# First matrices of two small networks: plain float32 products in four column quarters instead of split fp32r products

## The chip, the core and the metric

The kernel runs on one core of a Trainium2 chip. The core's engines each take their instructions in order from a queue of their own: TensorE (PE) multiplies matrices and keeps its result in PSUM, VectorE (DVE) and ScalarE (ACT) do arithmetic, GpSimd (POOL) does small work beside them, and SyncE (SP) issues the DMA transfers. An engine waits for another by a semaphore. PE's weight loads are shown as an engine of their own, PEld. The metric is the device time of one execution in microseconds (us), as the median of several runs.

## The reference, cut to what matters

A model of two blocks runs over 256 positions of 1024 channels in float32. The first block does, for each of two layers, a gated feed-forward, a mixing stage with three kinds of attention, and a second feed-forward. The second block (gated linear attention, attention on a memory, a mixture of experts) is not touched by the change. In the mixing stage one kind of attention reads compressed keys and values:

```
blocks = t[:, cmp_idx] + cmp_pos[:, None, :]                     # 15 blocks of 32 positions
blocks = blocks.transpose(0, 3, 1, 2, 4).reshape(B, G, n_cmp, CMP_LEN * Dh)   # G=2 groups, 2048 long
return jax.nn.silu(blocks @ w1) @ w2                             # w1: 2048 x 256, w2: 256 x 64
kc = rms_norm(compress(k_cmp, cmp_k_w1, cmp_k_w2), k_norm)
vc = compress(v_cmp, cmp_v_w1, cmp_v_w2)
```

So there are two small networks per layer, one for keys and one for values. Each multiplies 30 rows (2 groups x 15 blocks) of length 2048 with a first matrix of 2048 x 256, which is 2 MB.

## The kernel before

**Weights.** All weights stream from memory in units of at most 128 x 1024 numbers (512 KB), in the order of a list of requests (`mixing_requests`, L726, for a mixing stage). A request names a matrix, its first column, its width and, optionally, more. `load_ahead` (L265) issues a unit's DMA as soon as a room is free. `pump` (L277) splits loaded units in order: ACT writes the high part `whi` in the format fp32r (L311), DVE the rest `wlo` = raw - `whi` (L285), and the raw room becomes free. There are 5 rooms for raw units and 14 for the halves of 7 split units (`ST`); rooms that no split unit wants are given to the raw units (`wanted_spare`, L253). A unit marked as whole is not split: it stays in its raw room, `Taken.whole` (L338) hands it out, and `close` (L344) frees the room after its last product. Before the change only the experts' weights are whole; `pump` does not split ahead over a whole unit that is still open.

**Products.** An ordinary product of an activation block with a weight block is three fp32r matmuls, high by high, high by low, low by high (`mm3`, L357 to L360). `linear` (L386) goes over a request's units and both halves of the positions, and calls `tick` after each. Whole units are multiplied in plain float32, and the experts (L1936, L1961) put two products into the two halves of PE's 128 columns. Compressed values (L957) use quarters of 32 columns.

**The order of the work.** Every engine's order is the order in which the Python program issues instructions. Side work is written as generators. `tick` (L95) moves each running generator on to its next `yield`, starts at most one queued generator whose predecessors have ended, and lets `pump` split one unit. So the side work of a tick stands on PE, DVE and ACT between two pieces of the main products.

**The mixing stage.** The main line multiplies w_in in the requests D, E, F, B, A, C (L1162 to L1171), whose generators `post_D` to `post_C` normalize and transpose. `blocks` (L858) builds for each network the matrix X of its 16 blocks of 128 rows and 30 columns, and splits X as well (L890 on ACT, L891 on DVE). Then come `hidden(Xk)` and `hidden(Xv)` (L895), the products with the first matrices, 4 units each:

```python
for k in W.ks(u):
    for i, w in enumerate(W(k)):        # whi, wlo
        nc.tensor.matmul(p, X[0][k // 8][:, k % 8 * 60:k % 8 * 60 + 60], w, ...)
```

The stationary operand has 60 columns: the 30 of X's high part and the 30 of its low part, interleaved. The 60 rows of the result are added in pairs by a product with the constant `sums` (L915, in `squashed`, L908), between ACT's copy L911 and the silu (L918, L921). `compressed_keys` (L923) goes on with L929, L933 to L946, `compressed_values` (L950) with L957 and DVE's L960. After `hidden` come the gate products (`gate`, L1183: 8 ticks each, four of them), and beside them, one started per tick, four `sliding` (L1069 first), two `compressed` (L1011 first) and sixteen `selected_window` generators. The PSUM banks of the tags `mm`, `tp` and `accB` are two each. `finish(*heads)` at L1222 waits in ticks until they have all ended; then the merge follows.

**Small things.** Ring tiles (`ring`, L739) are eight buffers of 128 x 512. `sums` is made on POOL in the first feed-forward (L683 to L687).

Of the kernel before, what the change touches and what calls it, by code (L numbers as in the profile page):

```python
# [10 lines left out]
FT = mybir.dt.float32  # L11
FR = mybir.dt.float32r
I32 = mybir.dt.int32
AF = mybir.ActivationFunctionType
OP = mybir.AluOpType
# [54 lines left out]
def the_kernel(  # L70
# [115 lines left out]
    @contextmanager  # L186
    def stream(raw_slots, unit_bufs, requests):

        with tc.tile_pool(name="w", bufs=1, reuse_waits="tile") as wp:
            units, asked = [], []
            for w, c0, n, *pool in requests:
                ws = w if isinstance(w, tuple) else (w,)
                kt = ws[0].shape[0] // P
                per = min(kt, UNIT // n)
                asked.append((len(units), -(-kt // per) * len(ws), per, kt, n, len(ws)))
                for i, k0 in enumerate(range(0, kt, per)):
                    for m in ws:  # L200
                        units.append((m, c0, n, k0, min(per, kt - k0), bool(pool) and i % 4 in pool[0],
                                      isinstance(w, tuple)))
            now.update(room=unit_bufs, units=units, asked=asked, loads=[], parts=[], half=[], closed=0, open=0, busy=[])
            x_rooms[:] = [(wp, f"x{h}", True) for h in range(NH)]
            place_x()
            now["spare"] = [(wp, f"w{i}", True) for i in range(2 * unit_bufs)]
            with rooms(wp, raw_slots):
                yield
            assert not asked and now["closed"] == len(units)
# [67 lines left out]
    def pump(most=1, hurry=False, upto=None):  # L277


        units, parts, half = now["units"], now["parts"], now["half"]  # L280

        def second():
            if half:
                _, r, hi, lo, eng, at = half.pop()
                eng.tensor_sub(lo, r, hi.bitcast(FT))  # L285
                now["busy"].remove(at)
                used(at)

        load_ahead()
        while len(parts) < len(units) and (most > 0 if upto is None else len(parts) <= upto):  # L290
            *_, on_pool, whole = units[len(parts)]
            if len(parts) == len(now["loads"]):
                assert upto is None, "no room"
                break
            if whole:
                parts.append(None)
                continue
            if upto is None and any(whole for *_, whole in units[now["closed"]:len(parts)]):
                break
            if len(now["spare"]) < 2 + 2 * (upto is None):  # L300
                assert upto is None, "no room"
                break
            if hurry and not on_pool:
                return
            second()
            r, at = now["loads"][len(parts)]
            m, n = r.shape[1:]
            mine = [now["spare"].pop(0) for _ in range(2)]
            hi, lo = (block(at2, [UNIT], FR, t)[:, :m * n].rearrange("p (k n) -> p k n", n=n)
                      for at2, t in zip(mine, ("whi", "wlo")))  # L310
            nc.scalar.activation(hi, r, AF.Copy)  # L311
            half.append((len(parts), r, hi, lo, nc.gpsimd if on_pool else nc.vector, at))
            parts.append((hi, lo, mine))
            now["open"] += 1
            most -= 1
            load_ahead()
        if upto is None and most > 0 and not hurry or upto is not None and half and half[0][0] == upto:
            second()
# [321 lines left out]
    def mixing_constants(fb, tmp):  # L640
# [6 lines left out]
        dmul = fb.tile([P, P], FT, name="dmul")  # L647
        dadd = fb.tile([P, P], FT, name="dadd")
        rowm = fb.tile([P, 1], FT, name="rowm")
        sums = fb.tile([60, 30], FT, name="sums")  # L650
        mine = fb.tile([P, 4], FT, name="mine")
        nsink = fb.tile([P, 8], FT, name="nsink")
        pcp = fb.tile([P, 2, 16], FT, name="pcp")
# [7 lines left out]
        def load():  # L661
# [18 lines left out]
            nc.gpsimd.affine_select(rowm, rowm, pattern=[[0, 1]], compare_op=OP.is_ge, fill=0.0, base=-(CMPL - 1),  # L680
                                    channel_multiplier=1)

            nc.gpsimd.memset(sums, 1.0)  # L683
            nc.gpsimd.affine_select(sums, sums, pattern=[[-2, 30]], compare_op=OP.is_ge, fill=0.0, base=0,
                                    channel_multiplier=1)
            nc.gpsimd.affine_select(sums, sums, pattern=[[2, 30]], compare_op=OP.is_ge, fill=0.0, base=1,
                                    channel_multiplier=-1)  # L687
            nc.gpsimd.memset(mine, 1.0)
            nc.gpsimd.affine_select(mine, mine, pattern=[[-32, 4]], compare_op=OP.is_ge, fill=0.0, base=0,
                                    channel_multiplier=1)  # L690
# [35 lines left out]
    def mixing_requests(l):  # L726
        W = w_in[l]
        gate = lambda b, j: (W, 2584 + b * D + j * 512, 512)
        up = lambda j: [(w[l], j * 512, 512) for w in (w_up_nsa, w_up_sb, w_up_swa)]
        return [(W, 1304, 512), (W, 1816, 512), (W, 2328, 256), (W, 512, 512), (W, 0, 512), (W, 1024, 280),  # L730
                (nsa_cmp_k_w1[l], 0, 256), (nsa_cmp_v_w1[l], 0, 256), *(gate(b, 0) for b in range(3)), gate(0, 1),
                *up(0), gate(1, 1), gate(2, 1), *up(1), *square(w_out[l])]

    def mixing(l, cs, xt, rs, ready, start):
        nbias, tri, nones, dmul, dadd, rowm, sums, mine, nsink, pcp = cs
        nxt = start()
        with tc.tile_pool(name=f"mix{l}", bufs=1, reuse_waits="tile") as mp:

            def ring():  # L739
                return mp.tile([P, 512], FT, name="gt", tag="gt", bufs=8)  # L740
# [117 lines left out]
            def blocks(c, into, *after):  # L858
                while any(g in active for g in after):
                    yield  # L860
                X = ring()[:, :480].rearrange("p (j n) -> p j n", n=30)
                T2 = ring()[:, :256].rearrange("p (g m) -> p g m", g=NG)
                kds = []
                for h in range(NH):
# [18 lines left out]
                        nc.vector.tensor_add(X[:, 8 * o:8 * o + 8, g * NCMP:(g + 1) * NCMP], v,  # L883
                                             pcp[:, 8 * o:8 * o + 8, None].to_broadcast([P, 8, NCMP]))
                yield
                both = [mp.tile([P, 512], FR, name="gt", tag="gt", bufs=8)[:, :480] for _ in range(2)]
                for i, t in enumerate(both):

                    xh, xl = (t.rearrange("p (j n a) -> p j n a", n=30, a=2)[:, :, :, a] for a in range(2))
                    nc.scalar.activation(xh, X[:, 8 * i:8 * i + 8], AF.Copy)  # L890
                    nc.vector.tensor_sub(xl, X[:, 8 * i:8 * i + 8], xh.bitcast(FT))  # L891
                into.append(both)
                yield

            def hidden(X):  # L895

                W = Taken()
                p = bank("accB")[:60, :256]
                for u in range(W.count):
                    for k in W.ks(u):  # L900
                        for i, w in enumerate(W(k)):
                            nc.tensor.matmul(p, X[0][k // 8][:, k % 8 * 60:k % 8 * 60 + 60], w, start=i == k == 0,
                                             stop=i == 1 and k == W.kt - 1)
                    W.close(1)
                    tick()
                return p

            def squashed(p, o):  # L908

                half = t2()[:60, :256]  # L910
                nc.scalar.activation(half, p, AF.Copy, scale=0.5)  # L911
                yield
                tp = tbank()[:, :2, :30]
                for i in range(2):
                    nc.tensor.matmul(tp[:, i], half[:, i * P:(i + 1) * P], sums, start=True, stop=True)  # L915
                yield
                th = t2()[:, :60].rearrange("p (c n) -> p c n", n=30)
                nc.scalar.activation(th, tp, AF.Tanh)  # L918
# [1203 lines left out]
```

## Time and profile before

| | us |
|---|---|
| median of 3 runs | 2220.94 |
| lowest and highest run | 2216.73, 2223.05 |
| the profiled execution | 2218.42 |
| its span, first to last instruction | 2216.7 |
| mean granted clock of TensorE | 0.993 of full |
| mixing stage of layer 0, the part from request C on | from 275 us |
| the same of layer 1 | from 900 us |

In a row of the timeline the columns are the start, the time taken (from the first start to the last end, where several are merged), the engine, the line, the operation, what it writes and reads, its shape, how many, and in brackets the engine's idle time before it with what ended it. A matmul's time goes on after the next one has started, so the rate is read from starts.

### The profile page before, as it was taken

Reading aid. Unit: us, or ns where it says so; the run is one execution under the profiler, and the core shown is the slowest. Engines: PE = TensorE matmul, PEld = TensorE weight load, DVE = VectorE, ACT = ScalarE, POOL = GpSimd, SP = SyncE. Lnnn points to the kernel's source line nnn. Section 1 sums busy time; section 2 is a strip of 40 time slices with the busy share of each in tenths; the row PEclk is TensorE's granted clock in tenths of the full one; section 3 lists DMA queues with packets and bytes.
Section 4 is the critical chain, followed back from the end, with each engine's and each line's share of the span. In section 5 each row is a group of like instructions: output and inputs, shape, how many; then the busy total and the mean of one; then the engine's idle time right before and its main releaser. Section 6 shows DMA issues by size and latency. Waiting matters only on the chain. (4 is left out here: it accounts for less than half of the span.)

```text
span 2216.7 us, 29473 instructions
## 1 busy us (share of the span) xinstructions
PE 2132.8 (96%) x11117; PEld 1569.8 (71%) x11117; DVE 1139.0 (51%) x2022; ACT 910.7 (41%) x1448; POOL 177.0 (8%) x230
## 2 busy tenths in 40 slices
PE   8999989999999999899999999998999999989997
PEld 7778878788888888788788887873333687953332
DVE  6545786654554547875554457651111558441112
ACT  5435655454454447564544454531111454421111
POOL 1000200200000002101100001101000102010000
PEclk9999999999999999999999999999999999999999
DMA  7655553555546555535666464778998946589996
GB/s 249 195 177 153 163 153 110 175 183 186 181 156 210 188 172 154 162 105 158 224 205 194 153 186 159 249 251 307 393 394 300 353 126 219 185 308 381 395 393 246
DMA packets 240076, 490.49 MB, mean 221 GB/s; under 512 B 17538, under 2 KB 44850, under 8 KB 239922
## 3 DMA queue, kind: packets, MB, share of 16 engines
q1 hardware_dynamic: 239634, 487.42, 65.1%
q8 instruction: 92, 1.51, 0.3%
q10 hardware_dynamic: 288, 1.05, 0.1%
q14 instruction: 62, 0.51, 0.1%
HBM read 487.34 MB, written 1.07 MB: 220 GB/s over the span
## 5 line engine op out<-in xcount | busy, mean ns | idle before, releaser
L285 DVE TENSOR_TENSOR wlo<-raw,whi 128x1024 fp32r<-128x1024 f32 x524 | 633.8, 1227 | 300.7 <-ACT whi L311 297.9
L311 ACT ACTIVATE whi<-raw 128x1024 fp32r<-128x1024 f32 x524 | 540.7, 1051 | 299.8 <-PE tp L360 117.5
L1936 PE MATMUL mm<-raw,xg 128*64 128x512 f32 x1024 | 242.7, 602 | 7.9 <-PEq L1992 7.2
L358 PE MATMUL accB<-whi,xt 128*128 128x512 f32 (+3 forms) x448 | 176.2, 393 | 0.0
L360 PE MATMUL accB<-whi,xt 128*128 128x512 f32 (+3 forms) x448 | 166.0, 370 | 0.0
L359 PE MATMUL accB<-wlo,xt 128*128 128x512 f32 (+3 forms) x448 | 165.8, 370 | 0.0
L1936 PEld LDWEIGHTS mm<-raw,xg 128*64 128x64 f32 x1024 | 69.6, 137 | 132.8 <-issue 121.5
L358 PE MATMUL tp<-whi,xt 128*128 128x512 f32 (+1 forms) x384 | 143.4, 373 | 0.0
L360 PE MATMUL tp<-whi,xt 128*128 128x512 f32 (+1 forms) x384 | 143.4, 373 | 0.0
L359 PE MATMUL tp<-wlo,xt 128*128 128x512 f32 (+1 forms) x384 | 142.7, 372 | 0.0
L358 PE MATMUL mm<-whi,xt 128*128 128x512 f32 (+1 forms) x320 | 121.0, 378 | 1.4 <-DVE nbias L720 0.7
L1961 PE MATMUL mm<-raw,t 128*64 128x512 f32 x512 | 119.3, 607 | 0.5 <-DMA raw<-in_w_down_dram 0.5
L360 PE MATMUL mm<-whi,xt 128*128 128x512 f32 (+1 forms) x320 | 118.3, 370 | 0.0
L359 PE MATMUL mm<-wlo,xt 128*128 128x512 f32 (+1 forms) x320 | 117.7, 368 | 0.0
L1941 ACT ACTIVATE t<-mm 128x512 f32<-128x512 f32 x32 | 19.1, 597 | 187.5 <-PE mm L1936 187.5
L360 PEld LDWEIGHTS accB<-whi,xt 128*128 128x128 f32 x448 | 84.5, 189 | 15.1
L358 PEld LDWEIGHTS accB<-whi,xt 128*128 128x128 f32 x448 | 84.6, 189 | 13.6 <-issue 1.0
L359 PEld LDWEIGHTS accB<-wlo,xt 128*128 128x128 f32 x448 | 84.8, 189 | 11.8
L1870 DVE TENSOR_SCALAR back<-tp 128x256 fp32r<-128x256 f32 x32 | 13.6, 424 | 149.2 <-PE tp L1867 149.2
L610 DVE SCALAR_TENSOR_TENSOR t<-tp,ss,t 128x512 f32<-128x512 f32 (+1 forms) x48 | 33.8, 704 | 104.2 <-PE tp L360 104.2
L359 PEld LDWEIGHTS tp<-wlo,xt 128*128 128x128 f32 x384 | 72.1, 188 | 13.5
L360 PEld LDWEIGHTS tp<-whi,xt 128*128 128x128 f32 x384 | 72.1, 188 | 13.2
(520 smaller groups left out, 4007.7 us busy)
## 6 DMA issues: line engine op xcount, KB each, us to landing
raw<-in_w_gate_dram SPq DMA_DIRECT2D x128, 512.0 KB
raw<-in_w_up_dram SPq DMA_DIRECT2D x128, 512.0 KB
raw<-in_w_down_dram SPq DMA_DIRECT2D x128, 512.0 KB
raw<-in_w_in_dram SPq DMA_DIRECT2D x120, 512.0 KB
raw<-in_ffn_w_gate_dram SPq DMA_DIRECT2D x88, 512.0 KB
raw<-in_ffn_w_up_dram SPq DMA_DIRECT2D x88, 512.0 KB
raw<-in_ffn_w_down_dram SPq DMA_DIRECT2D x88, 512.0 KB
raw<-in_w_out_dram SPq DMA_DIRECT2D x32, 512.0 KB
```

The costliest lines, as they stand in the source:

```text
L285: eng.tensor_sub(lo, r, hi.bitcast(FT))
L311: nc.scalar.activation(hi, r, AF.Copy)
L358: nc.tensor.matmul(o, xh, wh, start=first, stop=False)
L359: nc.tensor.matmul(o, xh, wl, start=False, stop=False)
L360: nc.tensor.matmul(o, xl, wh, start=False, stop=last)
L610: nc.vector.scalar_tensor_tensor(ss[h], o, factor(h), ss[h], op0=OP.mult, op1=OP.mult)
L1870: nc.vector.tensor_scalar(bk, tp, 0.0, None, op0=OP.is_gt)
L1936: nc.tensor.matmul(p[half(i)], xgs[e // 4][k // 4][:, k % 4, e % 4], W.whole(k, i), start=k == 0, stop=k == KD - 1)
L1941: nc.scalar.activation(c[e], p, AF.Copy)
L1961: nc.tensor.matmul(p[half(j)], uu[e][:, f], W.whole(f)[:, j * 512:(j + 1) * 512], start=f == 0, stop=f == 3)
```

## The change

The two first matrices are requested with the mark "alone": their units are not split, but `pump` goes on splitting units behind them. `hidden` multiplies the raw blocks in plain float32. The four blocks k of a unit go to four quarters of 32 columns, so that the result has 128 rows, four partial sums of 32 rows, and it ticks after every second unit. X is kept whole, 32 columns wide, with the last two set to zero by POOL; its split and the two ring tiles for it are gone, and with them the last `yield` of `blocks`. `squashed` works on 128 rows, and `sums` becomes a 128 x 32 matrix that adds the four quarters, made from the identity matrix by one DVE reduction.

```diff
@@ stream
-                        units.append((m, c0, n, k0, min(per, kt - k0), bool(pool) and i % 4 in pool[0],
-                                      isinstance(w, tuple)))
+                        units.append((m, c0, n, k0, min(per, kt - k0), False, "alone" if pool else isinstance(w, tuple)))
@@ pump
-            if upto is None and any(whole for *_, whole in units[now["closed"]:len(parts)]):
+            if upto is None and any(whole is True for *_, whole in units[now["closed"]:len(parts)]):
                 break
@@ mixing_constants
-        sums = fb.tile([60, 30], FT, name="sums")
+        sums = fb.tile([P, 32], FT, name="sums")
...
-            nc.gpsimd.memset(sums, 1.0)
-            nc.gpsimd.affine_select(sums, sums, pattern=[[-2, 30]], compare_op=OP.is_ge, fill=0.0, base=0,
-                                    channel_multiplier=1)
-            nc.gpsimd.affine_select(sums, sums, pattern=[[2, 30]], compare_op=OP.is_ge, fill=0.0, base=1,
-                                    channel_multiplier=-1)
+            nc.vector.tensor_reduce(sums, ident.rearrange("p (i n) -> p n i", n=32), axis=AX.X, op=OP.add)
@@ mixing_requests
-                (nsa_cmp_k_w1[l], 0, 256), (nsa_cmp_v_w1[l], 0, 256), *(gate(b, 0) for b in range(3)), gate(0, 1),
+                (nsa_cmp_k_w1[l], 0, 256, "alone"), (nsa_cmp_v_w1[l], 0, 256, "alone"), *(gate(b, 0) for b in range(3)), gate(0, 1),
@@ blocks
-                X = ring()[:, :480].rearrange("p (j n) -> p j n", n=30)
+                X = ring().rearrange("p (j n) -> p j n", n=32)
+                nc.gpsimd.memset(X[:, :, 30:], 0.0)
...
-                both = [mp.tile([P, 512], FR, name="gt", tag="gt", bufs=8)[:, :480] for _ in range(2)]
-                for i, t in enumerate(both):
-
-                    xh, xl = (t.rearrange("p (j n a) -> p j n a", n=30, a=2)[:, :, :, a] for a in range(2))
-                    nc.scalar.activation(xh, X[:, 8 * i:8 * i + 8], AF.Copy)
-                    nc.vector.tensor_sub(xl, X[:, 8 * i:8 * i + 8], xh.bitcast(FT))
-                into.append(both)
-                yield
+                into.append(X)
@@ hidden
-                p = bank("accB")[:60, :256]
+                p = bank("accB")[:, :256]
                 for u in range(W.count):
-                    for k in W.ks(u):
-                        for i, w in enumerate(W(k)):
-                            nc.tensor.matmul(p, X[0][k // 8][:, k % 8 * 60:k % 8 * 60 + 60], w, start=i == k == 0,
-                                             stop=i == 1 and k == W.kt - 1)
+                    for i, k in enumerate(W.ks(u)):
+                        nc.tensor.matmul(p[32 * i:32 * i + 32], X[0][:, k], W.whole(k), start=u == 0,
+                                         stop=u == W.count - 1)
                     W.close(1)
-                    tick()
+                    if u % 2:
+                        tick()
@@ squashed
-                half = t2()[:60, :256]
+                half = t2()[:, :256]
...
-                    nc.tensor.matmul(tp[:, i], half[:, i * P:(i + 1) * P], sums, start=True, stop=True)
+                    nc.tensor.matmul(tp[:, i], half[:, i * P:(i + 1) * P], sums[:, :30], start=True, stop=True)
```

## Rows read from the trace of the kernel before

**Rows 1.** The page, part 1: busy time, share of the span, instructions.
```profile
PE 2132.8 (96%) x11117; PEld 1569.8 (71%) x11117; DVE 1139.0 (51%) x2022; ACT 910.7 (41%) x1448; POOL 177.0 (8%) x230
```
**Rows 2.** Busy time by stretch of the span, with granted clock, DMA share and GB/s.
```profile
core 0: us, PE busy (x) PEld busy (x) DVE busy (x) ACT busy (x) POOL busy (x), PEclk, DMA share, GB/s
270.00:282.00 12.00, 10.31 (x80) 9.26 (x79) 11.03 (x23) 5.24 (x11) 4.12 (x2) 1.00 0.27 88
282.00:300.00 18.00, 14.16 (x111) 12.38 (x110) 17.07 (x43) 12.36 (x28) 3.42 (x3) 1.00 0.68 197
300.00:312.00 12.00, 10.18 (x77) 7.79 (x76) 10.02 (x42) 6.44 (x23) 0.63 (x2) 0.94 0.59 190
...
895.00:907.00 12.00, 10.32 (x81) 9.29 (x80) 11.06 (x22) 5.24 (x12) 4.11 (x2) 1.00 0.31 89
907.00:925.00 18.00, 15.23 (x109) 13.76 (x108) 16.86 (x45) 12.03 (x28) 2.42 (x3) 0.91 0.72 214
925.00:937.00 12.00, 10.18 (x80) 7.65 (x78) 10.05 (x42) 6.35 (x23) 0.61 (x2) 1.00 0.52 161
...
330.00:360.00 30.00, 30.00 (x190) 25.05 (x189) 24.49 (x99) 19.12 (x57) 0.00 (x0) 1.00 0.33 106
```
**Rows 3.** PE's waits from 270 to 312 us: total, times, longest.
```profile
PE tp L433 <- DVE t L757: 1.3, 1, 1.3
PE tp L915 <- ACT t L911: 1.2, 1, 1.2
PE mm L1011 <- DVE vc L960: 1.2, 1, 1.2
PE mm L929 <- DVE HT L921: 1.0, 1, 1.0
PE mm L1069 <- DVE kc L934: 0.9, 1, 0.9
PE tp L994 <- DVE kcT L946: 0.7, 1, 0.7
PE accA L1144 <- ACT gt L1133: 0.6, 1, 0.6
PE tp L873 <- DVE qT L818: 0.3, 1, 0.3
```
**Rows 4.** Timeline of PE: `hidden`'s records, first and 24th, and two of layer 1.
```profile
284.38 0.36 PE L902 MATMUL accB<-whi,gt 128*60 128x256 f32 x1
287.17 0.28 PE L902 MATMUL accB<-wlo,gt 128*60 128x256 f32 x1
...
919.00 0.42 PE L902 MATMUL accB<-whi,gt 128*60 128x256 f32 x1
919.21 0.42 PE L902 MATMUL accB<-wlo,gt 128*60 128x256 f32 x1
```
**Rows 5.** Plain float32: one line's records, its weight loads in time, L957's records by stretch.
```profile
L1936 PE MATMUL mm<-raw,xg x1024: 592/592/1116, 1502.3 to 2192.5; 128*64 128x512 f32 x171
...
1600.98 0.14 PEld L1936 LDWEIGHTS mm<-raw,xg 128*64 128x64 f32 x2 [0.28 <-issue]
1601.41 0.14 PEld L1936 LDWEIGHTS mm<-raw,xg 128*64 128x64 f32 x2 [0.29 <-issue]
...
307.79:308.02 0.23, 0.22 (x16) 0.22 (x16) 1.00 0.22 80
```
**Rows 6.** The page, part 5: the splits (count, busy, mean ns, idle before).
```profile
L285 DVE TENSOR_TENSOR wlo<-raw,whi 128x1024 fp32r<-128x1024 f32 x524 | 633.8, 1227 | 300.7 <-ACT whi L311 297.9
L311 ACT ACTIVATE whi<-raw 128x1024 fp32r<-128x1024 f32 x524 | 540.7, 1051 | 299.8 <-PE tp L360 117.5
```
**Rows 7.** Timelines of DVE (first two) and ACT.
```profile
276.06 0.73 DVE L891 TENSOR_TENSOR gt<-gt 128x240 fp32r<-128x240 f32 x2 [0.81 <-ACT gt L890]
276.70 0.69 DVE L757 TENSOR_TENSOR t<-t,hr 128x512 f32<-128x512 f32 x1
...
288.23 2.94 ACT L311 ACTIVATE whi<-raw 128x1024 fp32r<-128x1024 f32 x3
```
**Rows 8.** A memset on POOL (ns min/median/max).
```profile
L796 POOL MEMSET HV<- x2: 198/198/198, 214.8 to 839.6; 128x128 f32 x2
```
**Rows 9.** One more stretch, columns as in rows 2.
```profile
309.80:313.50 3.70, 3.70 (x14) 2.68 (x14) 2.77 (x10) 1.67 (x4) 0.00 (x0) 0.62 0.01 2
```

## The prediction

> **What bounds the kernel now.** I read the page first. TensorE (PE) is busy for 96% of the span [rows 1], so a change pays if it takes PE time away or fills an idle stretch of PE. Then I cut the two mixing stages, one per layer, into stretches [rows 2]. Between 330 and 360 us, where the gates are multiplied, PE has no idle time at all. Before that it has: PE is busy 10.31 of 12 us, 14.16 of 18 and 10.18 of 12 in layer 0, and 10.32 of 12, 15.23 of 18, 10.18 of 12 in layer 1. That is 7.3 and 6.3 us idle, and these are the stretches the change edits. In the middle one of layer 0 DVE is busy 17.07 of 18 us, so DVE queues there, and PE waits for what stands in that queue. The list of PE's waits over the same 42 us names eight of them, 7.2 us in all [rows 3]: seven end on DVE or on ACT work that itself stood behind splits or DVE. The DMA engines are busy 0.27 to 0.72 of these stretches and are named in none of the waits. The bound is thus PE, plus short chains through a full DVE.
>
> **Part 1, the products of `hidden` (PE).** Before, each network does 16 blocks k, each twice (high and low part of the weights), so 32 fp32r records of 256 columns, 64 in a layer. The first run of 24 starts at 284.38 and its 24th at 287.17 us [rows 4], which is 0.121 us each, so 7.8 us in layer 0. In layer 1, twelve of them run at half clock, 0.21 us apart [rows 4], so 7.8 + 12 x 0.09 = 8.9 us. Together 16.7 us.
>
> After, each k is one plain float32 product. A plain product shows as two records: `into` of the experts makes 16 products for an expert, 512 in the kernel, and the trace has 1024 [rows 5]. Its record of 512 columns takes 0.43 us of stream, and two column halves run at once: a pair of weight loads starts every 0.43 us [rows 5]. So a record of 256 columns streams 0.215 us. What matters is how many quarters run at once. The nearest row is `compressed_values`, which already puts 32-column products into four quarters: 16 records of 64 columns fit into 0.22 us [rows 5]. By the same rule one such record streams 0.43/8 = 0.054 us; four at a time gives 4 x 0.054 = 0.22 us, two at a time would start the last one at 7 x 0.054 = 0.38 us. So four do run at once, though there all four quarters read the same moving data, and here each reads another block of the weights. I take four: 64 records in a layer are 16 groups of 0.215 = 3.45 us, and 0.1 for each of two restarts makes 3.65 us, 7.3 for both layers. The saving is 16.7 - 7.3 = 9.4 us. Bounds: two at a time (the most the trace shows with different moving data) 14.2 us, a saving of 2.5; one at a time 28 us, a loss of 11.
>
> The Trainium skill, page "TensorE: Matmul & The Clock Gate", section "Measured speedup vs the span model", gives 2.38 times for three column tiles of 512 columns, not 3. If four quarters lose in that proportion, a group takes 0.215 x 3/2.38 = 0.27 us by that estimate, and the saving would be 7.6 us in place of 9.4. Here the 16 records in 0.22 us [rows 5] speak for the full factor.
>
> **Part 2, the splits (ACT and DVE).** Eight units per layer are no longer split: eight `whi` of 1.05 us on ACT and eight `wlo` of 1.23 us on DVE [rows 6], that is 8.4 and 9.8 us. The block matrices' own splits go too, two ACT and two DVE instructions per network; the DVE pair is the 0.73 us row of L891 [rows 7]. What this is worth is what PE no longer waits. To see the order I counted ticks in the code: every tick moves each running generator on by one `yield`, and `hidden` now ticks after every second unit, so a layer has four ticks fewer, and the work of the chains moves between the gate products, which give about 1.4 us of PE per tick. Wait by wait [rows 3]:
> - L433 for L757 (1.3) and L873 for L818 (0.3): in DVE's queue L891 and the 0.81 us that it waits for ACT stand right before L757 [rows 7]. Both are gone, and they are longer than the wait. The turn of the V blocks comes one tick earlier (`blocks` has one yield less) and takes a `tp` bank between the two L433, so I leave 0.3.
> - L1144 for L1133 (0.6): the cover before it shrinks from 24 old records (2.8 us) to 12 groups (2.6), the DVE queue by the V split of 0.72. I leave 0.
> - L915 for L911 (1.2): three `whi` in a row, 2.94 us, stand before it on ACT [rows 7]. By the count only two units are split in the four ticks of `hidden`. I leave 0.3.
> - L929 for HT (1.0), L1069 for kc (0.9), L994 for kcT (0.7): each gets a gate product between its step and the next. I leave 0.5 for the three.
> - L1011 for vc (1.2): this moves. The first `sliding` is started one tick before L957 runs and holds one of the two `mm` banks, so the second half of L957 must wait until DVE has read the first, and the next L1069 must wait again. I take 1.6, between 0.6 and 2.4.
>
> That leaves 2.7 of 7.2 us in layer 0 and the same in layer 1 (of 6.3): a saving of 8.1 us. Bounds: 13.5 if all go; 0 if all stay, because the cover in `hidden` shrinks as well. A new loss would need a queue that gets longer, and those of ACT and DVE only get shorter.
>
> **Part 3, the rest.** Whole units stay in their raw room until PE has used them. Rooms are 5 raw and 14 for splits. Stepping `load_ahead`, `pump`, `close` and `used` tick by tick: every K and V unit is loaded at least 13 ticks before its use, since spare rooms are given away when no split unit wants them; the first gate unit is loaded 12 ticks and split 8 ticks before its use, where it was 10 and 5. So neither DMA nor a split comes late, and I put 0. SP's queue keeps its order, the same bytes are loaded. The memset of X's two empty columns sits on POOL (0.198 us for a 128x128 one [rows 8]) among the `hr` powers; POOL is busy 3.42 of 18 us [rows 2], cost 0, or 0.2 per network if a power is waited for, 0.8 in all. `sums` becomes one DVE reduction in the first feed-forward, once, in place of three POOL instructions: 0, hidden behind PE, at most the 0.73 of the L891 pair. `squashed` has the same instructions on 128 instead of 60 partitions: 0.
>
> **The clock.** In layer 0 the granted clock drops right after the idle stretch (0.94 of full over 300 to 312, 0.62 over 309.8 to 313.5), and in layer 1 over 907 to 925 (0.91) [rows 2, 9]: a short time at the lower of the two levels, 1.2 in place of 2.4 GHz. The clock lost is 0.38 x 3.7 = 1.4 us and 0.09 x 18 = 1.6 us, the most that a drop can cost; 1.1 of layer 1's is in part 1 already. PE idles less afterwards, but its short stretches move. I count one drop left of two, so 0, within 1.6 either way.
>
> **The sum.** The profiled execution took 2218.4 us (span 2216.7). 9.4 + 8.1 = 17.5 us less gives 2200.9. The profiled time is 2.5 below the median of the three runs (2220.94), so a median of 2203 is what I predict.
>
> **The rivals.**
> (a) Quarters run two at a time, because each reads its own block of weights. For: no row has four different streams. Against: the 16 records in 0.22 us. Saving 2.5 + 8.1 = 10.6: 2210 as a median. By the Trainium skill's 2.38, weighed above, the time would be 1.8 us over the forecast, 2205; it lies between this rival and the forecast.
> (b) The chains set the pace: what PE saves in `hidden` it waits at L915, L957 and L1069. For: all the waits of [rows 3] end on another engine, and the matmuls that cover them shrink. Against: the splits in front of those steps go. Stalls as before, 9.4 alone: 2211.
> (c) The change doesn't relieve the queues: whole units hold raw rooms, the gates' loads start late and their splits come forced. One load of 512 KB at the 197 GB/s of that stretch [rows 2] is 2.7 us and its split 2.3, so some 5 us late per layer: 2213. My step through the rooms speaks against it.
> (d) Slower: the quarters run one after the other, since all four read moving data through one port, and no wait goes. 28 us for what took 16.7: 2218.4 + 11.3 = 2229.7, a median of 2232. It decides from (16.7 + 6.7)/128 = 0.18 us per record on; the rows show 0.014 us for a quarter of that length, 0.055 scaled to 256 columns.
>
> **How the numbers follow.** Forecast 0.72, with 2196 to 2208 of its own (waits all gone and no clock drop: 7 lower; half of the waits' saving and one more clock drop: 5 higher). (a) 0.09, (b) 0.12, (c) 0.04, (d) 0.03. A measurement tells about 0.3%, 6.7 us, from no change: faster means under 2214.3. Forecast and nearly all of (a), (b), (c) are there; where (a) or (c) meets (b) it is within. So faster 0.88, same 0.08, slower 0.04. The range reaches over (a) and (b): 2196 to 2213.
>
> **What would show it.** Part 1: starts of `hidden` in groups of four, 0.215 us apart; 0.43 would mean two at a time. Part 2: about 2.7 us of PE waits per layer, the largest at L957 or the L1069 after it; no wait at L915 over 0.5. DVE under 80% busy where it was 95%. Part 3: no wait of PE on `whi`, `wlo` or `raw` in the first gate. It is wrong if the first gate ends less than 6 us earlier than before in layer 0.

## The result and the profile after

| | before | after |
|---|---|---|
| median, us (runs) | 2221.99 (4) | 2190.79 (4) |
| lowest and highest run | 2216.73, 2223.74 | 2189.77, 2191.49 |
| the profiled execution | 2218.42 | 2191.49 |
| mean granted clock of TensorE | 0.993 | 0.995 |

The ratio is 0.9866, with a 95% interval of 0.9849 to 0.9883: the change takes away about 30 us. The forecast was 2203 with a range of 2196 to 2213, so the direction was right and the size too small; the time lies outside the range. Later groups of runs gave 2191.05 for the kernel after and 2218.5 to 2219.8 for the kernel before.

The page, parts 1 and 5, of the kernel after (compare [rows 1] and [rows 6]). From here on the lines of the kernel after have numbers up to 12 lower than the same lines before:

```profile
PE 2117.0 (97%) x11117; PEld 1554.0 (71%) x11117; DVE 1118.9 (51%) x1999; ACT 892.4 (41%) x1424; POOL 172.5 (8%) x231
...
L284 DVE TENSOR_TENSOR wlo<-raw,whi 128x1024 fp32r<-128x1024 f32 (+1 forms) x508 | 614.7, 1228 | 292.7 <-ACT whi L310 288.3
L310 ACT ACTIVATE whi<-raw 128x1024 fp32r<-128x1024 f32 (+1 forms) x508 | 525.1, 1052 | 293.3 <-PE tp L359 115.7
```

Sixteen splits on each of DVE and ACT are gone, and PE's busy time is 15.8 us shorter. The span is 26.9 us shorter, so some 11 us were idle time of PE.

The timeline of PE in layer 0, the records of `hidden` and what follows them (compare [rows 4]):

```profile
283.07 2.80 PE L890 MATMUL accB<-raw,gt 128*32 128x256 f32 x48
285.80 0.66 PE L1133 MATMUL accA<-gt,sv 128*64 128x128 f32 x8
...
287.01 1.07 PE L890 MATMUL accB<-raw,gt 128*32 128x256 f32 x16
288.01 0.33 PE L798 MATMUL tp<-ident,t 128*128 128x128 f32 x1
```

From start to next start the 64 records take 2.73 + 1.00 = 3.73 us, 0.057 us a record or 0.23 us for a group of four. Before, the same products took 8.1 us in layer 0, read in the same way: 3.00 for the first run of 24 records and about 1.02 for each of five runs of eight.

PE's waits of the kernel after, layer 0 (compare [rows 3]); layer 1 shows the same three with the same sizes. The columns are total, times, longest:

```profile
PE mm L1058 <- DVE vc L949: 0.5, 1, 0.5
PE mm L946 <- DVE vc L949: 0.5, 1, 0.5
...
PE tp L1020 <- DVE t L989: 0.3, 1, 0.3
```

Eight waits of 7.2 us have become three of 1.3 us. The busy time by stretch, layer 0, then one stretch of layer 1 (columns as in [rows 2]):

```profile
270.00:282.00 12.00, 12.00 (x93) 11.33 (x92) 11.36 (x27) 5.98 (x14) 3.35 (x3) 1.00 0.58 186
282.00:300.00 18.00, 16.91 (x169) 12.07 (x168) 13.97 (x45) 8.84 (x21) 3.04 (x4) 1.00 0.61 195
300.00:312.00 12.00, 11.73 (x74) 9.29 (x72) 11.52 (x49) 7.33 (x24) 0.00 (x0) 1.00 0.51 148
...
907.00:925.00 18.00, 17.73 (x106) 13.74 (x104) 16.65 (x67) 11.46 (x39) 0.00 (x0) 1.00 0.42 120
```

DVE is busy 13.97 of 18 us where it was 17.07, and the granted clock is 1.00 throughout, where the kernel before had 0.94 in layer 0 and 0.91 in layer 1.

**The account of the gain.** The same gate product stands in both traces, so its start before less its start after says how much has been gained up to there. Across the mixing stage this grows by 12.7 us in layer 0 (from 230 to 395 us of the kernel before) and by 11.4 us in layer 1 (from 860 to 1025 us). Three terms make it up. PE's own time in `hidden`, at full clock: 8.1 - 3.7 = 4.4 us in each layer. The waits: 7.2 - 1.3 = 5.9 and 6.3 - 1.3 = 5.0 us. The clock: each layer had one stretch of 3.4 us at the lower level, 1.2 in place of 2.4 GHz, of which half is lost, 1.7 us. That gives 12.0 and 11.1 us, 23.1 of the 24.1 measured. The remaining 2.8 us of the profiled pair lie outside the stages that were edited, and in this pair most of them are the clock. Stretches at half clock, the kernel before in the first fence (its first two lines are in the mixing stages, the others outside) and the kernel after in the second:

```profile
310.70:314.10 3.40, 3.40 (x12) 2.07 (x11) 2.66 (x8) 1.20 (x2) 0.00 (x0) 0.50 0.09 11
918.20:921.60 3.40, 3.40 (x19) 3.40 (x18) 3.37 (x6) 1.71 (x3) 0.00 (x0) 0.51 0.98 316
457.40:460.80 3.40, 3.40 (x11) 2.80 (x10) 3.40 (x7) 1.75 (x6) 0.00 (x0) 0.51 0.84 203
1501.90:1505.30 3.40, 2.96 (x8) 1.14 (x10) 0.00 (x0) 0.00 (x0) 2.36 (x4) 0.50 0.03 7
1717.00:1720.40 3.40, 3.40 (x10) 0.96 (x8) 0.69 (x1) 0.49 (x1) 0.00 (x0) 0.50 1.05 387
1751.10:1754.50 3.40, 3.40 (x18) 3.40 (x18) 3.26 (x5) 2.11 (x4) 2.38 (x3) 0.50 0.78 208
```

```profile
1056.00:1059.40 3.40, 3.40 (x10) 2.90 (x11) 3.40 (x9) 1.75 (x6) 2.41 (x9) 0.50 1.04 277
1475.80:1482.60 6.80, 4.98 (x12) 1.64 (x14) 0.00 (x0) 0.00 (x0) 2.37 (x4) 0.50 0.01 3
```

Before there is a fifth outside the mixing, at 1082 us, which answers to the one at 1056 us after. This part of the difference is not a fixed effect of the change. A second profiled execution of the same kernel after (e9 below) gains the same 12.7 and 11.4 us in the mixing stages, but outside them it has as much half clock as the kernel before, 17.0 us, with stretches at the counterparts of 457, 1717 and 1751 us:

```profile
445.00:448.40 3.40, 3.26 (x10) 2.78 (x11) 3.40 (x8) 1.75 (x6) 0.00 (x0) 0.50 0.84 239
1690.90:1694.30 3.40, 3.40 (x12) 1.23 (x12) 0.69 (x1) 0.60 (x1) 0.00 (x0) 0.50 1.05 387
1725.00:1728.40 3.40, 3.27 (x15) 3.28 (x16) 3.26 (x6) 2.04 (x4) 2.89 (x3) 0.50 0.97 341
```

Its span is still 26.1 us shorter than that of the kernel before; where the 2.0 us beyond the mixing stages come from is not known. The last 8 to 13 us of every profiled execution are at half clock as well, but PE has no work there.

### The profile page after: what moved, and what is told of

Same layout as the page of the kernel before. It is cut to its first block, busy times and chain, and to the rows that moved or that the text cites. A ratio compares the mean times of both kernels' runs of the same rounds, so it can differ in the third digit from the quotient of the medians.

```text
span 2189.8 us, 29392 instructions
## 1 busy us (share of the span) xinstructions
PE 2117.0 (97%) x11117; PEld 1554.0 (71%) x11117; DVE 1118.9 (51%) x1999; ACT 892.4 (41%) x1424; POOL 172.5 (8%) x231
## 5 line engine op out<-in xcount | busy, mean ns | idle before, releaser
L284 DVE TENSOR_TENSOR wlo<-raw,whi 128x1024 fp32r<-128x1024 f32 (+1 forms) x508 | 614.7, 1228 | 292.7 <-ACT whi L310 288.3
L310 ACT ACTIVATE whi<-raw 128x1024 fp32r<-128x1024 f32 (+1 forms) x508 | 525.1, 1052 | 293.3 <-PE tp L359 115.7
```

## The experiments

Three theories on what took the waits away, beside PE's own saving. **Q**: the queues of ACT and DVE are relieved of the splits. **T**: the ticks of `hidden`, one after every second unit, put the steps of the chains behind other gate products. **K**: idle stretches cost twice, since the granted clock falls behind them. For each kernel the table has the median, the ratio to the kernel before in the same group of runs, PE's waits in layers 0 and 1 (262 to 375 and 880 to 1000 us), the time at half clock in both mixing stages together (profiled execution), the gain across the two stages as measured above, and what the three terms give for it: PE's time in `hidden` saved, plus waits saved, plus half of the half-clock time saved, over both layers.

| kernel | us | ratio | waits | half clock | gain, layers 0 and 1 | three terms |
|---|---|---|---|---|---|---|
| before | 2218.5 to 2222.0 | | 7.2, 6.3 | 6.8 | | |
| after | 2190.8 | 0.9866 | 1.3, 1.3 | 0 | 12.7, 11.4 | 23.1 |
| e1, a tick after each unit | 2200.5 | 0.9912 | 4.0, 4.0 | 0 | 9.1, 7.7 | 17.7 |
| e2, splits kept | 2222.7 | 1.0016 | 9.5, 9.7 | 23.9 | -1.8, -3.0 | -5.5 |
| e3, products alone | 2218.9 | 0.9998 | 9.1, 8.5 | 20.5 | -1.4, -0.9 | -2.1 |
| e4, ticks alone | 2223.3 | 1.0019 | 7.4, 7.4 | 17.1 | -3.2, -3.1 | -6.5 |
| e5, two quarters at a time | 2196.2 | 0.9896 | 1.3, 1.3 | 0 | 9.0, 7.6 | 16.2 |
| e6, one quarter at a time | 2209.0 | 0.9961 | 1.3, 1.3 | 0 | 2.1, 0.8 | 2.4 |
| e7, one bank | 2186.9 | 0.9866 | 1.3, 1.3 | 0 | 13.1, 11.7 | 23.1 |
| e8, e3 with filling products | 2214.9 | 0.9989 | 4.6, 5.3 | 10.2 | 0.3, -0.4 | 2.9 |

For e8 the filling products, 7.8 us, are taken off PE's saving. The three terms meet the measured gain within 1.7 us in all kernels but e8 (3.0 apart). So the account holds for all but e8, and the experiments say what moves each term. Intervals of the ratios are about 0.001 either way for e2 to e4 and e8, 0.0015 for e1 and e5 to e7.

**e1: a tick after each unit.** The change with the old number of ticks:

```diff
-                    if u % 2:
-                        tick()
+                    tick()
```

> The changed kernel (2190.8 us median; 1.3 us of PE waits left per mixing stage), but with a tick after every unit of the two products, as before the change: only the tick rule is undone. Theory Q (the waits went because ACT's and DVE's queues got shorter): the chain steps come earlier but still find short queues, so 0 to 1.5 us more per layer: 2190 to 2194. Theory T (the waits went because the chain steps moved between gate products, 1.4 us of PE each): L915, L929, L1069, L1011 wait again, about 3 us per layer, and a clock drop may come back: 2196 to 2200.

2200.47 us, 0.9912 (0.9897 to 0.9926), 9.7 us over the kernel after. PE's waits in layer 0:

```profile
PE mm L999 <- DVE vc L948: 1.2, 1, 1.2
PE accA L1132 <- ACT gt L1121: 0.9, 1, 0.9
PE mm L1057 <- DVE kc L922: 0.7, 1, 0.7
PE tp L982 <- DVE kcT L934: 0.7, 1, 0.7
```

These are the waits for vc, kc, kcT and the exponential `gt` of [rows 3], at nearly their old sizes, with a queue that has no splits of K and V in it. Those for t (1.3 and 1.2) and HT (1.0) are gone. So the relief of the queues takes away one group of waits, and the ticks, once the queues are relieved, the other. The time lies at the upper end of what T forecast, and Q alone, with 2190 to 2194, is out.

**e2: products and ticks as after, splits kept.** The units are split again and X too, but PE multiplies only the high part of the weights; the low part is left out:

```diff
-                (nsa_cmp_k_w1[l], 0, 256, "alone"), (nsa_cmp_v_w1[l], 0, 256, "alone"), *(gate(b, 0) for b in range(3)), gate(0, 1),
+                (nsa_cmp_k_w1[l], 0, 256), (nsa_cmp_v_w1[l], 0, 256), *(gate(b, 0) for b in range(3)), gate(0, 1),
@@ hidden
-                        nc.tensor.matmul(p[32 * i:32 * i + 32], X[0][:, k], W.whole(k), start=u == 0,
+                        nc.tensor.matmul(p[32 * i:32 * i + 32], X[0][:, k], W(k)[0].bitcast(FT), start=u == 0,
```

> The changed kernel, but the sixteen units of the first matrices in a layer pair are split again (eight whi and eight wlo a layer, in the order and rooms of the kernel before), and X is split too; the products read the high part as plain float32 in four quarters, so the low part of the weights is left out of the result. Only the relief of ACT and DVE is undone. Theory Q: most waits return, 3 to 5 us per layer, with one clock drop or two: 2197 to 2204. Theory T: 2191 to 2194.

2222.65 us, 1.0016 (1.0007 to 1.0026): all of the gain is gone, and some more; neither theory had it that high. Three of PE's waits in layer 0, and the stretch behind them:

```profile
PE tp L1025 <- DVE t L994: 2.2, 1, 2.2
PE accB L358 <- DVE wlo L284: 1.8, 1, 1.8
PE tp L909 <- ACT t L905: 1.5, 1, 1.5
...
290.40:304.10 13.70, 11.38 (x46) 7.85 (x47) 8.59 (x19) 6.36 (x13) 1.92 (x2) 0.50 0.80 262
```

PE saves its 8.8 us at full clock over both layers, and yet for 13.7 us on end it runs at half clock. The wait for `wlo` is new: each tick lets `pump` split one unit, so with four ticks fewer, units can be unsplit when PE comes to them.

**e3: the products alone.** e2 with a tick after each unit, so only the products in quarters differ from the kernel before (and the low part of the weights is left out). Against e2:

```diff
-                    if u % 2:
-                        tick()
+                    tick()
```

> As the run with the splits kept, and a tick after every unit as well: what remains of the change is the quartered products alone (the low part of the weights is again left out). The measured term of the products is 10 us of PE, of which 1.1 is clock. If the waits of before all stay: 2210 to 2213. If the shorter products leave the chains less cover (my rival b), part of the 10 us is waited for again: 2213 to 2219.

2218.93 us, 0.9998 (0.9989 to 1.0007): no change that can be measured, though PE needs 8.8 us less at full clock. The two largest waits in layer 0, then four stretches (the first two in layer 0, the others in layer 1):

```profile
PE mm L922 <- DVE HT L914: 1.7, 1, 1.7
PE accA L1137 <- ACT gt L1126: 1.6, 1, 1.6
...
282.00:300.00 18.00, 12.49 (x107) 6.52 (x106) 17.02 (x42) 11.88 (x27) 3.35 (x3) 0.87 0.70 202
300.00:316.00 16.00, 14.18 (x92) 10.67 (x93) 11.76 (x47) 7.62 (x24) 0.71 (x2) 0.83 0.49 148
907.00:925.00 18.00, 13.26 (x113) 8.49 (x115) 17.18 (x41) 11.60 (x24) 2.23 (x2) 0.81 0.71 211
925.00:941.00 16.00, 14.18 (x102) 10.57 (x103) 13.30 (x50) 8.42 (x28) 0.81 (x2) 0.89 0.55 174
```

DVE is as full as before, 17.02 of 18 us, and sets the pace: the waits for HT and `gt` grow from 1.0 and 0.6 to 1.7 and 1.6 us, 4.1 us more in all over both layers. The granted clock does the rest: 0.87, 0.83, 0.81 and 0.89 over these 68 us are 10.2 us lost, where the kernel before lost 3.4. The runs agree: the mean clock is 0.9893 for e3 and 0.9922 for the kernel before in the same group, some 6.5 us more lost. So 8.8 - 4.1 - 6.9 is about -2 us. This is what rival (b) of the prediction describes, here with the splits kept and with the clock on top.

**e4: the ticks alone.** The kernel before, with one edit in `hidden`:

```diff
-                    tick()
+                    if u % 2:
+                        tick()
```

> The kernel before (2222.0 us), with a tick after every second unit of the two products and nothing else changed. Theory T: the waits at L915, L929, L1069 and L994 shrink by 3 us per layer: 2214 to 2217. Theory Q: the queues are as full as before, so 0 to 1 us per layer: 2219 to 2223. In both the share of the granted clock of each run tells whether the spread of the runs of before (2216.7 to 2223.7) is clock drops.

2223.26 us, 1.0019 (1.0011 to 1.0028), 0.2% slower. In layer 0 the waits for HT, kc, kcT and L911 are gone, as after the change, but two others stand in their place:

```profile
PE tp L1032 <- DVE t L1001: 2.2, 1, 2.2
PE accB L359 <- DVE wlo L285: 2.0, 1, 2.0
```

T alone falls: the waits that it named went, but the time did not come down. The ticks are worth 9.7 us when the splits are gone (e1 against after) and cost 4 us when they aren't (e4 against before, e2 against e3).

**e5 and e6: fewer quarters at a time.** The change, with the products in two quarters and in one; `sums` is cut to 64 and 32 rows.

```diff
-                        nc.tensor.matmul(p[32 * i:32 * i + 32], X[0][:, k], W.whole(k), start=u == 0,
+                        nc.tensor.matmul(p[32 * (i % 2):32 * (i % 2) + 32], X[0][:, k], W.whole(k), start=k < 2,
```

> The changed kernel with its products in two of the four quarters, so two at a time: 64 records a layer stream 0.108 us each, 7.1 us in place of 3.7 and about as long as the 8.1 of before. So PE's products are undone and the relief of the queues and the ticks stay. Theory Q (the relief carries the gain, and the products only add to it once the queues are short): 3.4 us more per layer than the changed kernel: 2196 to 2198. If the longer products also cover the 1.3 us of waits left: 2194 to 2196. If instead the products carry the gain: 2205 or more.

> The changed kernel with all products in one quarter, one at a time, my rival d made on purpose: 64 records of 0.216 us, 13.8 us a layer in place of 3.7. If PE sets the pace of this stretch once the queues are short: 10 us more per layer: 2208 to 2212. If the chains set it: 2200 or less.

2196.18 us (0.9896, 0.9881 to 0.9911) and 2209.04 us (0.9961, 0.9948 to 0.9975). The first run of 48 records and what follows it, e5 (first two lines), then e6:

```profile
282.89 5.38 PE L890 MATMUL accB<-raw,gt 128*32 128x256 f32 x48
288.19 0.66 PE L1133 MATMUL accA<-gt,sv 128*64 128x128 f32 x8
```

```profile
281.80 10.55 PE L890 MATMUL accB<-raw,gt 128*32 128x256 f32 x48
292.27 0.66 PE L1133 MATMUL accA<-gt,sv 128*64 128x128 f32 x8
```

A record costs 10.47/48 = 0.218 us one at a time, 0.110 two at a time and 0.057 four at a time. In e5 PE needs 7.2 us a layer for these products, little less than the 8.1 before, and still 22 us of the gain are there, as Q forecast (2196 to 2198). So relief and ticks together carry most of it. In e6 PE needs 14.0 us a layer, far more than before, and the kernel is still faster than before. From e5 to e6 PE's time grows by 13.8 us over both layers and the median by 12.9: with the queues relieved, PE's own time counts one for one, which it didn't in e3.

**e7: one bank for the compressed values.** Both groups of `compressed_values` go into one PSUM bank, so that the second doesn't wait for DVE to read the first.

```diff
+                both = bank("mm")
                 for g in range(NG):
-                    p = bank("mm")[:, :DH]
+                    p = both[:, g * DH:(g + 1) * DH]
```

> The changed kernel with both groups of the compressed values in one mm bank, and their two multiplications after both, to take away the one PE wait left in the middle of them (0.5 us, and 0.5 before the next sliding). If both waits go: 2 us less in all, 2188 to 2189.5. If the wait only moves to the next one that needs a bank: 2190 to 2191.5.

2186.89 us, 0.9866 (0.985 to 0.9881). The expectation of the time was met or passed, its reason was not. The waits in layer 0 are still 1.3 us; two have become one:

```profile
PE mm L1060 <- DVE vc L951: 1.0, 1, 1.0
```

The gain across the mixing stages is 0.7 us more than after's. The rest of the 4 us lies where nothing was edited; its profiled execution has one stretch of 3.4 us at half clock behind the mixing stages, that of the kernel after two of 10.2 us together. Its ratio is that of the kernel after, so it is not shown to be the better version.

**e8: e3 with filling products.** 17 fp32r products a layer (some 3.9 us), whose result nobody reads, right before four of the waits of e3; the low part of the weights is left out here too. One of the four places:

```diff
@@ compressed_keys
+                f = bank("accA")
+                for _ in range(5):
+                    nc.tensor.matmul(f, xt.at(0, 0)[0], xt.four(0, 0)[0], start=True, stop=True)
                 p = bank("mm")[:30, :DH]
```

> The products alone (2218.9 us, with five clock drops in its two mixing stages) with idle PE filled: 3 to 5 extra fp32r matmuls of 512 columns (0.23 us each, results unused) before each of the four places of a layer where PE waits longest; the low part of the weights is left out as there. Theory K (the idle stretches cost twice, since the granted clock falls after them): the drops of the mixing stages go, 1.5 us each: 2211 to 2216. Rival (the drops have another cause, and more PE work only adds): 2219 to 2223.

2214.9 us, 0.9989 (0.9979 to 0.9999), against 0.9998 for e3: with more work on PE it is not slower. The two ratios differ by 0.0009, about 2 us, and their intervals overlap. Three of the stretches of e3:

```profile
282.00:300.00 18.00, 16.49 (x115) 10.10 (x113) 15.99 (x34) 10.30 (x21) 3.25 (x2) 0.81 0.70 203
300.00:316.00 16.00, 14.75 (x111) 11.05 (x112) 14.13 (x55) 9.55 (x31) 0.81 (x2) 1.00 0.55 164
925.00:941.00 16.00, 15.30 (x115) 11.26 (x113) 14.32 (x56) 8.63 (x29) 0.81 (x2) 1.00 0.52 151
```

One of the three is still slow, two are at full clock; the fourth, from 907 us, has 0.91 for 0.81. In both mixing stages 10.2 us are at half clock where e3 has 20.5; that gives back 5.1 us and the filling costs part of it, so that the two stages end 2.2 us earlier than in e3. One execution of each could mislead, but the runs say the same: over eleven runs each, the mean granted clock is 0.9935 for e8 and 0.9893 for e3, which is 14 and 24 us of the span lost. K had all drops go, and only some went; the rival (2219 to 2223) is out. This supports K in the mixing stage.

**e9 and e10: the kernel after once more, and a filling at the entry into the experts.** There PE waits 4 to 5 us, and behind it the clock falls in both kernels. e10 puts 34 products of 256 columns right before that wait:

```diff
             while gs[0] in active:
                 tick(split=LS[1])
+            f = bank("mm")[:, :256]
+            for _ in range(34):
+                nc.tensor.matmul(f, xn[0][0][:, :P], picks[0][:, 0].rearrange("p e s -> p (e s)"), start=True, stop=True)
```

> The changed kernel as it is, with more runs on the chip of the next two, so that its mean granted clock can be set beside that of the other kernels. All theories: 2190 to 2192 us, mean clock 0.995 to 0.996. Theory K (idle stretches cost twice because the granted clock drops behind them) says that the span times the mean clock, the span that would be left at full clock, is about 2179.5 us, 20 below the 2199.7 of the kernel before, and that the clock takes about 9.5 us where it took 17: some 8 of the 28 to 31 us that the change gained are clock. If the clock has no part in the gain, the two losses are equal.

> The changed kernel, plus 34 fp32r products of 128x256 (4.3 us) whose result nobody reads, put on PE right before it waits 4.7 us for the entry into the experts, far from the mixing stages. There the granted clock was 0.5 for 6.8 us from 1475.8 on. Theory K: this drop goes, and 3.4 us with it, though PE does more: 2187 to 2188. Rival L (drops come at fixed distances whatever PE did before): the drop stays, 2190 to 2192. If the wait is counted from PE's last product, the experts start 4 us later: 2194 or, without the drop, 2191.

e9: 2191.05 us, mean clock 0.9954 over five runs; the eleven runs of the kernel before beside it have 0.9922. Of the mean spans, 2188.2 and 2216.5 us, the clock thus takes 10 and 17 us, and 2178 and 2199 would be left at full clock. That is close to what K forecast: some 7 of the 28 us gained are clock, and 21 are left for PE's own time and its waits. (Both clock figures include the half clock at the end of the span, where PE has no work.) The two drops of the mixing are 3.4 of the 7 (profiled execution); where the rest lies is not shown. e10: 2196.12 us (0.9901, 0.9886 to 0.9915), 5 us slower. The place in e9 (first two lines) and in e10; PEq, which ends the wait, is PE's own sequencer:

```profile
1469.10 4.01 PE L1834 MATMUL mm<-pick,xn 128*128 128x256 f32 x32
1476.96 11.62 PE L1925 MATMUL mm<-raw,xg 128*64 128x512 f32 x40 [3.85 <-PEq L1981]
```

```profile
1465.62 4.04 PE L1834 MATMUL mm<-pick,xn 128*128 128x256 f32 x32
1469.50 4.17 PE L1982 MATMUL mm<-pick,xn 128*128 128x256 f32 x34
1475.89 10.50 PE L1925 MATMUL mm<-raw,xg 128*64 128x512 f32 x40 [2.22 <-PEq L1984]
...
1476.20:1479.60 3.40, 3.40 (x10) 1.20 (x8) 0.00 (x0) 0.00 (x0) 1.92 (x4) 0.50 0.02 5
```

From the first gathering product to the first expert it is 7.9 us in e9 and 10.3 in e10: with the filling, 2.2 us of the wait still come after PE's last product, so the filling costs 2.4 us. The same lines run a second time, for the other layer of the second block, which the expectation did not count (68 records of them, not 34). There, e9 (first two lines), then e10:

```profile
1945.34 4.05 PE L1834 MATMUL mm<-pick,xn 128*128 128x256 f32 x32
1951.80 8.80 PE L1925 MATMUL mm<-raw,xg 128*64 128x512 f32 x40 [2.41 <-PEq L1981]
```

```profile
1944.58 4.05 PE L1834 MATMUL mm<-pick,xn 128*128 128x256 f32 x32
1948.47 4.18 PE L1982 MATMUL mm<-pick,xn 128*128 128x256 f32 x34
1954.59 7.95 PE L1925 MATMUL mm<-raw,xg 128*64 128x512 f32 x36 [1.94 <-PEq L1984]
```

From the gathering to the expert it is 6.5 us in e9 and 10.0 in e10, 3.5 us more. The two places together cost 5.9 us, which accounts for the 5. The drop at the first place is shorter, 3.4 for 6.8 us, but it stays. K's forecast (2187 to 2188) was wrong here, since the filling doesn't reach the end of the wait; it neither shows nor excludes that a full cover would keep the clock.

**e11: e7 with the same filling.**

> The changed kernel with both groups of the compressed values in one PSUM bank (it took 2186.9 us) and the same 34 filling products. Its drop at the experts' entry was 3.4 us long, so theory K gives 1.7 less, 2185; rival L gives 2186.9; if the wait is counted from PE's last product, 2189 to 2191.

2198.0 us, 0.9901 (0.9886 to 0.9916), the ratio of e10. It is 11 us over e7; by e10 the filling at its two places explains some 6 of them, and the rest is open. One bank is again not measurably better than two.

## Why the prediction was wrong in size

The mechanism held: products and waits both fell, and their savings added up. Two terms of the sum were too small. The waits were put at 8.1 us and measured 10.9, and the clock was put at nothing, within 1.6 us, and gave 2.3 more in the mixing stages alone. The forecast was 12 us above the measured median: 6.6 us of that lie in the mixing stages (24.1 for 17.5), 2.8 outside them, and some 3 come from the step between profiled execution and median.

**Part 1, the products: right.** Forecast 7.8 and 8.9 us before, 3.65 after, a saving of 9.4. Measured 3.73 a layer after and a saving of about 10 (1.1 of it the half clock of layer 1, as the prediction had said). The step from the 64-column records of [rows 5] to 256 columns held: four quarters that read four different blocks run at once. Rivals (a) and (d) are out by the starts alone, and e5 and e6 show what quarters that run two and one at a time would have cost: 5 and 18 us. The Trainium skill, page "TensorE: Matmul & The Clock Gate", section "Measured speedup vs the span model", gives 2.38 times for three column tiles; the estimate from it was 0.27 us for a group. The trace has 0.23, and from one quarter to four 0.218/0.057 = 3.8 times, so the measurement decides against that proportion for these plain float32 products.

**Part 2, the waits: right in kind, too small.** The forecast left 2.7 us a layer; 1.3 are left. The waits for t, L911, HT, kc and kcT went as said, and so did the signs named for them: DVE is busy 78% of the middle stretch, there is no wait at L915, and the largest waits are at the products that were L957 and L1069. What was mis-sized is the term for vc, 0.5 at L946 and 0.5 at L1058, where 1.6 was taken, and the rests, 1.1 in all, that were left at L433, at L915 and for HT, kc and kcT: none came, and 0.3 at L1020 was not foreseen. That makes 10.9 us saved for 8.1.

**The clock: a step that failed.** It was counted at 0 within 1.6 us, as one drop left of two. Both drops in the mixing went, 3.4 us in all (1.1 of them counted in part 1), so 2.3 us more than forecast. The price of a drop, 1.4 to 1.6 us, was nearly right (1.7); what was wrong was to let one stay because PE's short waits move: with 1.3 us of waits left in a layer, none stayed. In the mixing stages the drops go with PE's waits: before, e2, e3, e4 and e8, with 4.6 to 9.7 us of waits in a layer, all show them there; after, e9, e1, e5, e6 and e7, with 1.3 to 4.0 us, show none. In layer 0 of before, e2, e3 and e4 each drop begins within 1.5 us of the end of a wait of PE. That the waits cause them is supported by e8 and otherwise argued from this order: the kernels with drops are also the ones that keep the splits. Outside the mixing the profiled pair gains about 3 us more by the clock, since 457, 1717 and 1751 us have no drop after the change while that at the experts' entry is longer (6.8 us for 3.4), but e9 has three of these drops again. So whether the change moves the clock there is open (e10).

**Sum against sum.** Of the profiled difference, 26.9 us, the forecast had 17.5. Products give 0.6 more, waits 2.8, the clock in the mixing 2.3, the clock outside about 3 (in this pair of executions); under 1 us is left unexplained. In addition the 2.5 us between the profiled execution and the median of three runs were added, but in three later groups, 55 runs in all, the kernel before has medians of 2218.5, 2219.0 and 2219.8, so most of those 2.5 us were chance.

**The terms are not independent.** The prediction added part 1 and part 2 and put (b), in which the chains eat up the products' gain, at 0.12. In this change they did add, but only since the splits went too: the products alone give nothing (e3), the ticks alone cost 4 us (e4), both with the splits kept cost 4 us (e2), products with relief 18 us (e1), all three 28 to 31. The relief of ACT and DVE is what lets the other two count; relief without the other two was not run. The step of the prediction that said so, that the waits end on work behind splits, was the one that carried most of the gain.

**Part 3: right.** No wait of PE for `raw`, `whi` or `wlo` shows in the mixing of the kernel after, and (c) did not happen. In e2 and e4, where fewer ticks met the same number of splits, a wait of 1.8 to 2.0 us for `wlo` did come, and with the whole units (after) it does not.

## What to carry to other kernels

Before PE time is saved in a stage, look at which engine the waits around it end on: where DVE was busy 17 of 18 us here, the saved time turned into longer waits, and taking work off that engine was worth more than the matmuls. Cost a stage as PE time plus waits plus half of the time at half clock, and expect the drops to come and go with PE's waits, not as a constant. A yield or a tick that is moved has no price of its own: here fewer ticks were worth 9.7 us with relieved queues and cost 4 with full ones. Filling products that did not reach the end of the wait cost time (e10).

## What the runs showed of the hardware

Four plain float32 products of 32 columns each, with four different moving blocks of 256 columns, run at 3.8 times the rate of one (0.218 and 0.057 us a record).

The granted clock falls behind short waits as well as long ones. In e3 no wait in layer 0 is longer than 1.7 us, and three drops to 0.5, 3.4 us each, begin at 288.5, 298.7 and 312.4 us, right behind waits that end at 288.5, 298.1 and 310.9. The Trainium skill, page "TensorE: Matmul & The Clock Gate", section "A second HAM failure mode: psum-queue depth-cycling", describes a kernel in which frequent short idle times between groups of matmuls made the clock swing; e3's trace agrees, with idle times that end on DVE and ACT.

The spread of one kernel's runs is for a good part this clock: of 55 runs of the kernel before, the 10 with a mean clock of 0.991 have a mean span of 2218.1 us, 24 with 0.992 have 2217.5, 12 with 0.993 have 2215.4 and 7 with 0.994 have 2213.8. A drop at the same wait comes in one execution and not in another: PE waits 2.1 us for DVE's `x` at the end of layer 1's merge, near 1055 us, in the profiled executions of the kernel after, of e7 and of e9, and only the first has a drop behind it, although e9 is the same kernel.
